# Diagonal blocks and score order of a chunked RWKV-7 layer: 8 steps of blocks instead of 16, and one more score per step in place of four ahead of the first

## The chip, the cores and the metric

One core of a Trainium2 chip runs the whole program in one launch. The metric is the device time of that launch in microseconds. Every product is made on TensorE (PE) from fp32 operands; VectorE (DVE), ScalarE (ACT) and GpSimd (POOL) do the elementwise work, and SyncE (SP), ScalarE and GpSimd issue DMAs.

## The reference, cut to what matters

Two trunk layers over 1024 latent and 256 context tokens of width 1024: an even layer (RWKV-7 time mixing in both directions with 12 heads of 64, and a Fourier mix), then an odd layer (retention). The change touches only the RWKV recurrence of the even layer:

```
def step(s, inp):
    r_t, w_t, k_t, v_t, kk_t, b_t = inp
    sa = jnp.einsum('bhij,bhj->bhi', s, kk_t)
    s = s * w_t[:, :, None, :] - sa[..., None] * b_t[:, :, None, :] + v_t[..., None] * k_t[:, :, None, :]
    return s, jnp.einsum('bhij,bhj->bhi', s, r_t)
...
for d in range(2):
    s_ctx, yc = rwkv7_scan(*tc[:6], zeros, d == 1)
    _, yl = rwkv7_scan(*tl[:6], s_ctx, d == 1)
```

## The kernel before, in words

The recurrence is computed in chunks of 64 tokens. With 1280 tokens there are 20 chunks, and the 12 heads in two directions are cut into three groups, so there are 60 steps. A step works on four `x` (two directions, two pairs of heads) of two heads each. What a step needs is prepared earlier by phase A and stored in DRAM: `AR` and `BK` (operands), `VT` (values), `PC` (decays), `Y0` (a bonus term), `G` (gates).

For each step `s`:

- `scores(s)` (L1121, products at L1127) multiplies `BK` by `AR` into the PSUM tiles `psc`; `masked(s)` (L1129) masks them on VectorE into a tile `scr`. Loads of `arr` and `bkp` come from `load_ops` (L1091).
- The 64x64 triangular system of each head is solved by the inverses of its two 32x32 diagonal blocks and a correction between them. `diag(s)` (L1138) stores the diagonal blocks of two steps from `scr` to the DRAM tile `dn`; `gather(s)` (L1179) loads them into a tile `tl`, one block to a partition.
- `inv(m)` (L1208) inverts all 128 blocks of the eight steps 8m to 8m+7 at once, in 31 rows of a product (L1218) and a sum (L1220) each. For m=0 these run on VectorE, for all others on GpSimd. It then stores the result twice (`dz`, and transposed as `dx`, with a copy at L1225 between).
- `bring(q, ...)` (L1232) loads the inverses of four steps back on SyncE, `dx` into `scr` and `dz` into `zs`.
- In step s-1, `offd1` (L1244, product at L1252) and `offd2` make the correction for step s from `scr` and `zs`.
- In step s, TensorE makes `wu` (L1496), ScalarE copies it to `wt` (L1497), a second product, the update of the state (L1529 to L1535, where VectorE scales by `pc`) and the output `pyo` (L1542) follow. TensorE runs in program order, so whatever it waits for holds all that is written behind it.

Scores are made ahead of the steps: in each step one score of a later step (L1515), up to 19 steps ahead, and in the steps listed in `CU` a second one (L1570, `more`).

Before the first step there is the last piece of phase A, the gate projections (tiles 20 to 25). The generator of phase B runs beside them: scores of steps 0 to 7, then `blocks(s)` (L1161) for s = 8, 10, ..., 22. `blocks` computes only the diagonal 64x64 products of two steps, from `dka` and `dkb` (loaded by `blocks_load`, L1154, on SyncE), so that the inverses of m=1 and m=2 can run before the full scores of those steps exist. ScalarE copies the 32x32 blocks to `dg` and stores them to `dn`. `both()` (L1364) places rows of the inverses beside the gate products: m=0's on VectorE, m=1's on GpSimd.

Behind the gates come, in this order, the bring-back of m=0, the loads for step 0, four scores (steps 8 to 11, `PR` = 4, with `bky` as their operand tile and `psg` as extra PSUM), and the steps. The rows of an inverse are placed by ticks: `slot(j)` is called four times a step and emits 2, 1, 1 and 1 rows; a gather follows its last store by three ticks (`TD`), the rows follow the gather by two (`WT`). `rows_until(s + 1)` at the start of a step emits whatever rows and bring-backs that step's correction still needs. GpSimd also runs the output norms (`norm`, L1277): the power L1296 and the product L1298, five norms to a group of 20 steps.

These lines set the places that the change edits:

```
for s in range(E, EB, 2):
    blocks(s)
    both()
    yield
...
if ivs and st.tick >= ivs[0][2]:
    row()
...
if s in CU:
    more(s)
slot(3)
```

Of the kernel before, what the change touches and what calls it, by code (L numbers as in the profile page):

```python
# [10 lines left out]
F32 = mybir.dt.float32  # L11
# [12 lines left out]
NB = 3  # L24
# [15 lines left out]
AG = 1  # L40
AL = {43:(42,),44:(43,),45:(44,),46:(42,),47:(43,),48:(45,),49:(42,),50:(43,),51:(45,),52:(42,),53:(43,),54:(45,),55:(42,),56:(43,),57:(42,),58:(43,)}
NR = 2
CU = (1, 2, 3, 4, 5, 7, 9)
PR = 4
EB = 24
EP = 2
EZ = 1
ER = (2,1,2)
# [9 lines left out]
NY = 6  # L58
TT = 1
TS = 7  # L60
RW = (2,1,1,1)
# [963 lines left out]
def phaseB(g):  # L1025
    nc, tc = g.nc, g.tc
    mm = nc.tensor.matmul
# [23 lines left out]
    E = 8  # L1051
    PES, ACTS, DVES = "tensor", "scalar", "vector"
    H = [slice(0, 64), slice(64, 128)]
# [3 lines left out]
    PSC = [ps2.tile([128, 512], F32, name=f"psc{h}") for h in range(2)]  # L1057
# [23 lines left out]
    ex = ee.enter_context(tc.tile_pool(name="exB", bufs=1, reuse_waits="tile"))  # L1081
# [6 lines left out]
    def gtile(name):  # L1088
        return tail.gen.tile([128, 512], F32, tag="gen", name=name)

    def load_ops(s, bk=None):  # L1091
        if 0 <= s < NS:
            AR[s] = ARR[s % (L + 3)]
            st.q.dma_start(AR[s], g.D["AR"][s // 20][:, s % 20])
            BK[s] = BKP[s % NB] if bk is None else bk
            nc.sync.dma_start(BK[s], g.D["BK"][s // 20][:, s % 20])
# [57 lines left out]
    def blocks_load(s):  # L1154

        if s < EB:
            DA[s], DB[s] = (ex.tile([128, 2, 4, 64], F32, tag=t, name=f"{t}{s}", bufs=2) for t in ("dka", "dkb"))
            for o, n in ((DA, "AR"), (DB, "BK")):
                nc.sync.dma_start(o[s], g.D[n][s // 20][:, s % 20 : s % 20 + 2, :, 0:64])

    def blocks(s):  # L1161

        spread(s)
        c = s % 8
        for j in range(2):
            for x in range(4):
                for h in range(2):
                    mm(PSC[h][0:64, 256 * j + 64 * x : 256 * j + 64 * x + 64], lhsT=DB[s][H[h], j, x], rhs=DA[s][H[h], j, x], start=True, stop=True, tile_position=(64 * h, 0))
        dg = ex.tile([64, 2, 4, 2, 32], F32, tag="dg", name=f"dg{s}", bufs=2)
        for b in range(2):  # L1170
            bs = slice(32 * b, 32 * b + 32)
            for h in range(2):
                nc.scalar.copy(dg[bs, :, :, h].rearrange("p c x t -> p (c x) t"), PSC[h][bs].rearrange("p (a t) -> p a t", t=64)[:, :, bs])
            nc.scalar.dma_start(DN[s // 8][b, 8 * c : 8 * c + 16].rearrange("u s t -> s u t"), dg[bs].rearrange("s c x h t -> s (c x h) t"))
        if c % 4 == 2:
            dgs.append((s + 1, st.tick + TD))
        blocks_load(s + 4)

    def gather(s):  # L1179

# [169 lines left out]

    for s in range(NB):
        load_ops(s)
    for _ in range(EW):
        yield
    for s in range(E):
# [16 lines left out]
        else:  # L1372
            rows(EP)

    blocks_load(E)
    blocks_load(E + 2)
    for s in range(E, EB, 2):
        blocks(s)
        both()
# [65 lines left out]
    def more(s, ps=None):  # L1445

        if ns <= min(s + L, NS - 1):
            if s >= 0:
                fetch(s)
            scores(ns, ps)  # L1450
            scored(ps)
# [3 lines left out]
        bring(*back.pop(0))  # L1455
    load_v(0)
    load_late(0)

    while nl < E + PR:
        load_ops(nl, st.pd.tile([128, 2, 256], F32, tag="y", name=f"bky{nl}", bufs=NY).rearrange("p q t -> p (q t)").rearrange("p (x t) -> p x t", t=128))  # L1460
        nl += 1
    while back and back[0][0] < 2:
        bring(*back.pop(0))
    load_group(0)
    for i in range(PR):
        more(-1, [gtile(f"psg{i}_{h}") for h in range(2)] if i % 2 else None)
        if i == NB:
            st.q = nc.sync
            for nl in range(nl, nl + NB):
                load_ops(nl)  # L1470
            nl += 1
            st.q = nc.scalar
        rows(RW[i % 4])
    st.q = nc.sync
    rows_until(0)
    offd1(0)
# [774 lines left out]
```

## Time and profile before

| | us |
|---|---|
| median of 3 runs (lowest, highest) | 1906.62 (1893.33, 1909.16) |
| the profiled execution's own time | 1908.86 |
| its span in the profile | 1907.1 |
| TensorE busy in the span | 1721.7 (90%) |
| VectorE, ScalarE, GpSimd busy | 992.4, 707.8, 743.4 |
| stretch with the diagonal blocks | 618 to 650 |
| gates and first inverse to the end | 650 to 681 |
| space before the first step | 681 to 708 |
| the 60 steps | 708 to about 1155 |

The times of single operations come from the profiled execution, whose own time is 2.24 us above the median of the runs. The span is shorter than its time by 1.8 us, which lie around it. A step is counted from its copy at L1497 to that of the next step.

### The profile page before, as it was taken

The numbers are of one execution on the slowest core, as the hardware profiler recorded it, in microseconds if no ns is written. First come the engines' busy times: TensorE is split into PE (matmuls) and PEld (weight loads), VectorE is DVE, ScalarE is ACT, GpSimd is POOL, SyncE is SP. The second block draws the span as 40 slices with busy tenths as digits, with TensorE's granted clock in tenths as the row PEclk, the third lists the DMA queues.
The fourth block names the chain that finished last, engine by engine and source line by source line (L and its number), as shares of the span: only waits on it lengthen the run. The fifth ranks groups of instructions, "written<-read, shape, count | busy, mean of one in ns | idle before, by whom it ended". The sixth has DMA issues, their size and how long they took to land.

```text
span 1907.1 us, 40211 instructions
## 1 busy us (share of the span) xinstructions
PE 1721.7 (90%) x16706; PEld 1460.4 (77%) x16706; DVE 992.4 (52%) x1532; ACT 707.8 (37%) x1570; POOL 743.4 (39%) x827
## 2 busy tenths in 40 slices
PE   6999998989787858898888888999999999999898
PEld 4777776777665747787877766779899898898776
DVE  6532589888986455545452334553442433524543
ACT  5322454545431314565555454343221222212321
POOL 4331344444342285088778411122442414414300
PEclk9999999999889979999897887999999999999999
DMA  9562265546548777688776664432111101101162
GB/s 317 172 223 73 74 182 141 155 136 175 131 137 264 164 190 224 175 223 217 202 187 169 160 161 144 143 122 84 45 45 36 55 23 56 56 23 56 51 204 99
DMA packets 343370, 261.90 MB, mean 137 GB/s; under 512 B 110396, under 2 KB 293172, under 8 KB 342932
## 3 DMA queue, kind: packets, MB, share of 16 engines
q1 hardware_dynamic: 319252, 222.88, 41.5%
q10 hardware_dynamic: 19536, 20.72, 3.8%
q0 software_dynamic: 4400, 15.73, 2.3%
q8 instruction: 132, 2.16, 0.5%
q14 instruction: 50, 0.41, 0.1%
HBM read 181.36 MB, written 77.91 MB: 136 GB/s over the span
## 4 chain that ended last, share of the span: by engine, by line
PE 45%; POOL 7%; issue 5%; DMA 5%; DVE 5%; ACT 2%; SPq 0%; ACTq 0%; POOLq 0%; DVEq 0%
PE pv L1905 6%; PE pg L1849 5%; PE pq L1849 5%; PE pk L1849 5%; PE pow_oo L1644 4%; PE pow_eo L1644 3%; POOL zz L1220 2%; POOL tp L1218 2%; PE psc L1127 2%; PE pst L1995 2%; PE wu L1496 1%; DMA br<-scr_BK 1%; PE inc L1252 1%; PE pkc L1849 1%; PE wu L1510 1%
## 5 line engine op out<-in xcount | busy, mean ns | idle before, releaser
L533 PE MATMUL pgm<-hh,wh 128*128 128x512 f32 (+1 forms) x624 | 171.8, 385 | 0.0
L511 POOL TENSOR_TENSOR wl<-wr,wh 128x512 fp32r<-128x512 f32 x60 | 86.8, 1451 | 212.0 <-ACT wh L509 198.0
L533 PE MATMUL pgm<-hl,wh 128*128 128x512 f32 (+1 forms) x624 | 162.0, 369 | 0.0
L533 PE MATMUL pgm<-hh,wl 128*128 128x512 f32 (+1 forms) x624 | 161.6, 368 | 0.0
L1218 POOL TENSOR_TENSOR tp<-zz,tl 128x60 f32<-128x60 f32 (+23 forms) x217 | 111.4, 513 | 47.8 <-DMA tl<-dn 31.8
L1220 POOL TENSOR_TENSOR zz<-zz,tp 128x60 f32<-128x60 f32 (+23 forms) x217 | 119.8, 552 | 17.0
L533 PEld LDWEIGHTS pgm<-hl,wh 128*128 128x128 f32 x624 | 108.1, 197 | 20.5 <-POOL hl L469 0.7
L533 PEld LDWEIGHTS pgm<-hh,wl 128*128 128x128 f32 x624 | 107.9, 196 | 19.7
L533 PEld LDWEIGHTS pgm<-hh,wh 128*128 128x128 f32 x624 | 104.9, 198 | 21.0 <-issue 6.2
L1905 PE MATMUL pv<-wv,hh 128*128 128x256 f32 x640 | 117.2, 285 | 0.0
L556 DVE SCALAR_TENSOR_TENSOR m<-pgm,dv,m 128x255 f32<-128x255 f32 (+2 forms) x108 | 105.2, 987 | 11.2 <-ACT m L546 8.4
L1532 DVE TENSOR_TENSOR inc<-inc,state 128x256 f32<-128x256 f32 x54 | 23.4, 433 | 158.4 <-PE inc L1529 57.6
L1905 PEld LDWEIGHTS pv<-wv,hh 128*128 128x128 f32 x640 | 99.5, 192 | 0.1
L1133 DVE TENSOR_TENSOR scr<-psc,mask 128x512 f32<-128x512 f32 x116 | 74.3, 682 | 35.2 <-PE psc L1127 35.2
L1644 PE MATMUL pow_eo<-w_eo,yhw_eo 128*128 128x512 f32 x320 | 90.5, 404 | 0.4 <-ACT w_eo L1610 0.3
L1905 PE MATMUL pv<-wv,hl 128*128 128x256 f32 x320 | 90.5, 283 | 0.0
L1127 PE MATMUL psc<-arr,bkp 64*64 64x128 f32 x1792 | 71.2, 286 | 10.7 <-DVE scr L1133 5.6
L1296 POOL TENSOR_TENSOR rv<-rv,mhalf 128x8 f32<-128x8 f32 x15 | 24.8, 1652 | 138.6 <-DVE rv L1295 84.9
L820 POOL TENSOR_TENSOR ar<-m,Pp 128x640 f32<-128x640 f32 (+2 forms) x30 | 36.6, 1228 | 95.6 <-ACT Pp L812 91.0
L1644 PE MATMUL pow_oo<-w_oo,yhw_oo 128*128 128x512 f32 x256 | 73.6, 404 | 0.1
L1644 PEld LDWEIGHTS pow_eo<-w_eo,yhw_eo 128*128 128x128 f32 x320 | 60.8, 192 | 16.0 <-ACT w_eo L1610 1.1
L1849 PE MATMUL pg<-hh,wg 128*128 128x512 f32 x256 | 72.1, 393 | 0.0
(348 smaller groups left out, 4305.0 us busy)
## 6 DMA issues: line engine op xcount, KB each, us to landing
aw<-ada_w SPq DMA_DIRECT2D x16, 1024.0 KB, 10.4
wr<-w_ev SPq DMA_DIRECT2D x60, 256.0 KB, 4.1
scr_AR<-ar SPq DMA_DIRECT2D x24, 640.0 KB, 3.7
scr_BK<-bk SPq DMA_DIRECT2D x24, 640.0 KB, 4.5
br<-scr_BK ACTq DMA_DIRECT2D x60, 256.0 KB, 4.1
arr<-scr_AR SPq DMA_DIRECT2D x56, 256.0 KB, 4.4
bkp<-scr_BK SPq DMA_DIRECT2D x56, 256.0 KB, 4.0
x<-xin SPq DMA_DIRECT2D x20, 512.0 KB, 6.3
```

Of the source, the lines that this page charges most:

```text
L511: nc.gpsimd.tensor_tensor(out=wl, in0=wr, in1=wh.bitcast(F32), op=ALU.subtract)
L533: g.nc.tensor.matmul(ps[:, b, :n], lhsT=st[:, k % 4, :], rhs=mv[:, k, c0 : c0 + n], start=(k == 0 and i == 0), stop=(k == 7 and i == 2))
L556: nc.vector.scalar_tensor_tensor(out=o, in0=i, scalar=g.muc[:, q, ft : ft + 1], in1=o, op0=ALU.mult, op1=ALU.add)
L820: nc.gpsimd.tensor_tensor(out=ar[:, cs, 64:128], in0=ch(proc(self.r, d, lo, n)), in1=Pp[:, cs, 1:65], op=ALU.mult)
L1127: mm(ps[h][H[m], 128 * x : 128 * x + 128], lhsT=BK[s][H[h], x, H[m]], rhs=AR[s][H[h], x, :], start=True, stop=True, tile_position=(64 * h, ...
L1133: tt(out=out, in0=p.rearrange("p (d q t) -> p d q t", d=2, q=2), in1=K["mask2"].unsqueeze(2).broadcast_to([128, 2, 2, 128]), op=ALU.mult)
L1218: eng.tensor_tensor(out=tv, in0=ZZ[:, 0:k, s : s + 1].broadcast_to([U, k, n]), in1=TL[:, s : s + 1, s + 1 : 32].broadcast_to([U, k, n]), o ...
L1220: eng.tensor_tensor(out=zo, in0=zo, in1=tv, op=ALU.add)
L1644: self.g.nc.tensor.matmul(ps[:, 512 * b : 512 * b + 512], lhsT=st[:, k, :], rhs=mv[:, 512 * b : 512 * b + 512], start=(k == 0 and i == 0), ...
L1849: mm(ps[:, 512 * b : 512 * b + n], lhsT=st[:, k, :], rhs=mv[:, k, o : o + n], start=(k == 0 and i == 0), stop=(k == 7 and i == 2))
L1905: mm(ps[:, 256 * e : 256 * e + 256], lhsT=st[:, k, c0 : c0 + 128], rhs=mv[:, k, :], start=(k == 0 and i == 0), stop=(k == 7 and i == 2))
L1995: mm(ps[:, 128 * (i - i0) : 128 * (i - i0) + 128], lhsT=o.kz[d][:, t], rhs=o.v[:, t], start=True, stop=True)
```

## The change

`EB` goes from 24 to 16, so that `blocks` runs for s = 8, 10, 12, 14 only (m=1). The blocks of m=2 (steps 16 to 23) now come from the scores themselves, by `diag`, as those of all later steps do. `PR` and its loop go, with the `bky` and `psg` tiles; the scores of steps 8 to 11 are made inside the steps, as `CU` now holds 0 to 10 instead of 1, 2, 3, 4, 5, 7 and 9. In `blocks` the four 64x64 quadrants of the array take one head and one step each, where before the two steps followed each other in one half of the columns; `dg` is 128 partitions wide, two copies of 128x256 take the place of four of 32x256, and four stores that of two. The loads of blocks 8 and 10 are issued by SyncE ahead of the first scores; those of blocks 12 and 14 by ScalarE behind the stores.

```diff
-CU = (1, 2, 3, 4, 5, 7, 9)
-PR = 4
-EB = 24
+CU = tuple(range(11))
+EB = 16
...
-                nc.sync.dma_start(o[s], g.D[n][s // 20][:, s % 20 : s % 20 + 2, :, 0:64])
+                st.q.dma_start(o[s], g.D[n][s // 20][:, s % 20 : s % 20 + 2, :, 0:64])
...
+        for x in range(4):
+            for h in range(2):
+                for j in range(2):
+                    mm(PSC[h][H[j], 64 * x : 64 * x + 64], lhsT=DB[s][H[h], j, x], rhs=DA[s][H[h], j, x], start=True, stop=True, tile_position=(64 * h, 64 * j))
+        dg = ex.tile([128, 4, 2, 64], F32, tag="dg", name=f"dg{s}", bufs=2)
+        for h in range(2):
+            nc.scalar.copy(dg[:, :, h], PSC[h][:, 0:256].rearrange("p (x t) -> p x t", t=64))
         for j in range(2):
-            for x in range(4):
-                for h in range(2):
-                    mm(PSC[h][0:64, 256 * j + 64 * x : 256 * j + 64 * x + 64], lhsT=DB[s][H[h], j, x], rhs=DA[s][H[h], j, x], start=True, stop=True, tile_position=(64 * h, 0))
-        dg = ex.tile([64, 2, 4, 2, 32], F32, tag="dg", name=f"dg{s}", bufs=2)
-        for b in range(2):
-            bs = slice(32 * b, 32 * b + 32)
-            for h in range(2):
-                nc.scalar.copy(dg[bs, :, :, h].rearrange("p c x t -> p (c x) t"), PSC[h][bs].rearrange("p (a t) -> p a t", t=64)[:, :, bs])
-            nc.scalar.dma_start(DN[s // 8][b, 8 * c : 8 * c + 16].rearrange("u s t -> s u t"), dg[bs].rearrange("s c x h t -> s (c x h) t"))
+            for b in range(2):
+                u0, r0 = 8 * (c + j), 64 * j + 32 * b
+                nc.scalar.dma_start(DN[s // 8][b, u0 : u0 + 8].rearrange("u s t -> s u t"), dg[r0 : r0 + 32, :, :, 32 * b : 32 * b + 32].rearrange("s x h t -> s (x h) t"))
         if c % 4 == 2:
             dgs.append((s + 1, st.tick + TD))
+        st.q = nc.scalar
         blocks_load(s + 4)
+        st.q = nc.sync
...
     for s in range(NB):
         load_ops(s)
+    blocks_load(E)
+    blocks_load(E + 2)
     for _ in range(EW):
         yield
...
-    blocks_load(E)
-    blocks_load(E + 2)
     for s in range(E, EB, 2):
         blocks(s)
         both()
...
-    while nl < E + PR:
-        load_ops(nl, st.pd.tile([128, 2, 256], F32, tag="y", name=f"bky{nl}", bufs=NY).rearrange("p q t -> p (q t)").rearrange("p (x t) -> p x t", t=128))
+    for _ in range(NB):
+        load_ops(nl)
         nl += 1
     while back and back[0][0] < 2:
         bring(*back.pop(0))
     load_group(0)
-    for i in range(PR):
-        more(-1, [gtile(f"psg{i}_{h}") for h in range(2)] if i % 2 else None)
...
-        rows(RW[i % 4])
     st.q = nc.sync
     rows_until(0)
     offd1(0)
```

In SyncE's order between the first inverse and the first step, the kernel before has four `bky` loads behind the first value load `vu0` and ahead of the bring-back of steps 4 to 7 (`scr4`, `scr6`, `zs1`) and the decays `pc0`:

```order
L1104 DMA vu0_5632<-scr_VT_61 64x1024
L1096 DMA bky8_5637<-scr_BK_65 128x512
L1096 DMA bky9_5640<-scr_BK_65 128x512
L1096 DMA bky10_5643<-scr_BK_65 128x512
L1096 DMA bky11_5646<-scr_BK_65 128x512
L1237 DMA scr4_4620<-dx0_5511 32x16x32
L1237 DMA scr6_4621<-dx0_5511 32x16x32
```

At the same place of SyncE's order the changed kernel has the loads of the three `bkp` tiles:

```order
L1103 DMA vu0_5509<-scr_VT_61 64x1024
L1095 DMA bkp2_4609<-scr_BK_65 128x512
L1095 DMA bkp0_4607<-scr_BK_65 128x512
L1095 DMA bkp1_4608<-scr_BK_65 128x512
L1239 DMA scr4_4620<-dx0_5398 32x16x32
L1239 DMA scr6_4621<-dx0_5398 32x16x32
```

Three loads stand where four stood; the bring-back and the `pc0` loads stay behind them.

In GpSimd's order, the kernel before ends m=2's inverse (`zz1`, then `dz2`, the copy to `tl2`, `dx2`) ahead of the first norm of step 10 (`rv0_0`, `cg0_0`), and m=3 begins behind that norm:

```order
L1220 TENSOR_TENSOR zz1_4631<-zz1_4631,tp1_4633 128x31
L1224 DMA dz2_6302<-zz1_4631 128x1024
L1225 COPY tl2_4626<-zz1_4631 64x32x32
L1227 DMA dx2_6305<-tl2_4626 64x1024
L1296 TENSOR_TENSOR rv0_0_7076<-rv0_0_7076,mhalf_77 128x8
L1298 TENSOR_TENSOR cg0_0_6990<-cg0_0_6990,rv0_0_7076 128x512
L1213 MEMSET zz1_4631 128x1024
```

In the changed kernel the same norm stands on GpSimd amid m=2's inverse, which reads `tl2`:

```order
L1220 TENSOR_TENSOR tp1_4633<-zz1_4631,tl2_4626 128x220
L1222 TENSOR_TENSOR zz1_4631<-zz1_4631,tp1_4633 128x10x22
L1298 TENSOR_TENSOR rv0_0_6901<-rv0_0_6901,mhalf_77 128x8
L1300 TENSOR_TENSOR cg0_0_6803<-cg0_0_6803,rv0_0_6901 128x512
L1220 TENSOR_TENSOR tp1_4633<-zz1_4631,tl2_4626 128x231
L1222 TENSOR_TENSOR zz1_4631<-zz1_4631,tp1_4633 128x11x21
```

Ten of the 31 rows of m=2 now stand ahead of the norm and 21 behind it, then `dz2`, the copy and `dx2`. Further on, the norm `rv0_512` stands behind 14 rows of m=3 (21 before) and `rv0_768` behind 29 of them (behind `dx3` before).

## Rows read from the trace of the kernel before

**Rows 1.** Windows, 618 to 650 us: busy of each engine, TensorE's clock, DMA share, GB/s
```profile
618.00:650.00 32.00, 24.30 (x313) 19.67 (x314) 6.66 (x20) 11.33 (x34) 1.28 (x1) 0.89 0.93 202
```

**Rows 2.** Timeline of TensorE, diagonal blocks (start, duration, idle before and its releaser)
```profile
622.53 1.77 PE L1168 MATMUL psc<-dka,dkb 64*64 64x64 f32 x32 [5.02 <-DMA dkb<-scr_BK]
...
638.38 1.15 PE L1168 MATMUL psc<-dka,dkb 64*64 64x64 f32 x32 [2.09 <-DMA dkb<-scr_BK]
...
648.52 1.15 PE L1168 MATMUL psc<-dka,dkb 64*64 64x64 f32 x32 [0.38 <-DMA dkb<-scr_BK]
```

**Rows 3.** Timeline of ScalarE, a pair of copies of one diagonal block
```profile
644.74 0.63 ACT L1173 COPY dg<-psc 32x256 f32<-32x256 f32 x2 [0.38 <-ACT dg L1173]
```

**Rows 4.** Timeline of VectorE, a gate amid the first inverse, and the inverse's last operation
```profile
649.15 0.69 DVE L601 SCALAR_TENSOR_TENSOR gth<-gth,pgb 128x512 f32<-128x512 f32 x1 [3.76 <-ACT gth L600]
...
680.51 0.21 DVE L1220 TENSOR_TENSOR zz<-zz,tp 128x31 f32<-128x31 f32 x1
```

**Rows 5.** Timeline of TensorE, the first of the four scores ahead of step 0
```profile
698.03 1.98 PE L1127 MATMUL psc<-arr,bky 64*64 64x128 f32 x32 [20.46 <-DMA bky<-scr_BK]
```

**Rows 6.** Timeline of SyncE, the issue of the two pc loads
```profile
700.75 1.25 SPq L1114 DMA_DIRECT2D pc<-scr_PC  x2
```

**Rows 7.** Timeline of ScalarE, the copy of wu, one per step: steps 1, 6 to 10, 15, 18, 23
```profile
713.31 0.37 ACT L1497 COPY wt<-wu 128x256 f32<-128x256 f32 x1
...
753.39 0.37 ACT L1497 COPY wt<-wu 128x256 f32<-128x256 f32 x1 [1.13 <-DMA bkp<-scr_BK]
...
759.57 0.37 ACT L1497 COPY wt<-wu 128x256 f32<-128x256 f32 x1 [0.22 <-PE wu L1496]
...
767.47 0.37 ACT L1497 COPY wt<-wu 128x256 f32<-128x256 f32 x1 [2.79 <-PE wu L1496]
...
772.78 0.37 ACT L1497 COPY wt<-wu 128x256 f32<-128x256 f32 x1 [0.21 <-PE wu L1496]
...
784.31 0.37 ACT L1497 COPY wt<-wu 128x256 f32<-128x256 f32 x1 [6.43 <-PE wu L1496]
...
814.37 0.37 ACT L1497 COPY wt<-wu 128x256 f32<-128x256 f32 x1 [0.20 <-PE wu L1496]
...
837.12 0.37 ACT L1497 COPY wt<-wu 128x256 f32<-128x256 f32 x1 [0.82 <-PE wu L1496]
...
866.86 0.37 ACT L1497 COPY wt<-wu 128x256 f32<-128x256 f32 x1 [1.28 <-PE wu L1496]
```

**Rows 8.** Timeline of GpSimd, end of m=2's inverse, two norms, m=3's inverse
```profile
744.92 0.53 POOL L1227 DMA_DIRECT2D dx<-tl  x1 [0.29 <-POOL tl L1225]
792.39 1.67 POOL L1296 TENSOR_TENSOR rv<-rv,mhalf 128x8 f32<-128x8 f32 x1 [46.94 <-DVE rv L1295]
...
810.56 0.24 POOL L1218 TENSOR_TENSOR tp<-zz,tl 128x31 f32<-128x31 f32 x1 [14.28 <-DMA tl<-dn]
...
820.98 0.60 POOL L1218 TENSOR_TENSOR tp<-zz,tl 128x231 f32<-128x231 f32 x1
...
826.74 0.66 POOL L1218 TENSOR_TENSOR tp<-zz,tl 128x255 f32<-128x255 f32 x1
...
838.65 1.65 POOL L1296 TENSOR_TENSOR rv<-rv,mhalf 128x8 f32<-128x8 f32 x1 [1.61 <-DVE rv L1295]
...
841.38 0.59 POOL L1218 TENSOR_TENSOR tp<-zz,tl 128x220 f32<-128x220 f32 x1
...
852.09 0.27 POOL L1220 TENSOR_TENSOR zz<-zz,tp 128x31 f32<-128x31 f32 x1
...
855.65 0.53 POOL L1227 DMA_DIRECT2D dx<-tl  x1 [0.29 <-POOL tl L1225]
```

**Rows 9.** DMA issues by transfer: count, size of each, median us from issue to landing
```profile
scr<-dx SPq DMA_DIRECT2D x30, 64.0 KB, 5.5
...
dx<-tl POOLq DMA_DIRECT2D x6, 256.0 KB, 4.0
...
pc<-scr_PC SPq DMA_DIRECT2D x6, 20.0 KB, 3.5
```

More of the change, by code (lines that the diff above doesn't have):

```diff
@@ L1464, in phaseB @@
     load_group(0)
-    for i in range(PR):
-        more(-1, [gtile(f"psg{i}_{h}") for h in range(2)] if i % 2 else None)
[L1467 to L1472, printed above, removed]
-        rows(RW[i % 4])
     st.q = nc.sync
```

## The prediction

> **What bounds the kernel now.** I read the busy times in windows first. In the 32 us in which the kernel before computes its diagonal blocks (618 to 650), TensorE is busy for 24.30 us, the DMA engines for 0.93 of the time, VectorE for only 6.66 us [rows 1]. Then TensorE's timeline of that stretch: block 8 waits 5.02 us and the block at 638.38 waits 2.09 us, both for a `dkb` load, while a block itself takes 1.15 us or somewhat more [rows 2]. So the blocks stage runs at the pace of its loads. ScalarE's rows show the other cost of a block: a pair of copies takes 0.63 us and the pair before held it for 0.38 us [rows 3]. VectorE shows what the stage ends with: the first inverse (m=0, steps 0 to 7) still waits 3.76 us for a gate at 649.15, and then runs nearly without a gap to 680.72 [rows 4]. Nothing of the RWKV steps can start before that inverse.
>
> Behind it, TensorE idles for 20.46 us until the `bky` loads land, and then makes four scores (steps 8 to 11) before the first step [rows 5]; SyncE issues the two `pc` loads only at 700.75 [rows 6]. Then I read the start of each step from ScalarE's copy of `wu` (L1497), one row per step: a step with a second score takes 7.90 us (step 7: 767.47 - 759.57), one without takes 5.31 to 6.18 (steps 8 and 6) [rows 7]. Last I read GpSimd: m=2's inverse (steps 16 to 23) hands over its result at 744.92 and is needed in step 15 (814.37), so it has 69 us in hand; m=3's runs from 810.56 to 852.36 and is needed in step 23 (866.86) [rows 7, 8]. The slack of m=2 is what the change spends.
>
> **Blocks and gates: -9 us.** Four blocks (16 to 22) go with their loads and copies. TensorE loses four blocks of at least 1.15 us, 4.6 us (638.38 is the first of the four, 648.52 the last), and the 2.09 and 0.38 us of waits among them; the loads of blocks 8 and 10 are issued before the first scores, which takes the 5.02 us [rows 2]. That is 12.1 us. Against it: blocks 12 and 14 are loaded by ScalarE behind two copies and four stores of their predecessor, so that the load is asked for later; I charge 2 us, the size of the wait at 638.38. Left: 10.1. The inverse on VectorE moves with the gates that its rows stand between, so its start moves by as much, but its later part is bare work (649.76 to 680.72) that no gate shortens, and GpSimd's m=1 starts earlier beside it and slows it sooner; I take 9 of the 10.1. Bounds: 15 if the wait of 3.76 us goes too [rows 4], 3 if the loads are as late as now. The four-at-a-time form itself I cost at nothing: the trace has 32 matmuls to a block [rows 2] and the changed kernel as many.
>
> One rule speaks against this term. The trace has the DMA engines at 0.93 busy there [rows 1]. By the Trainium skill, "DMA: Bandwidth & Descriptors", section "Issuing engines are not separate DMA queues", transfers started by ScalarE or SyncE run on the same 16 engines, and another issuer saves only issue time. By it the loads of blocks 12 and 14 gain nothing from ScalarE; the sum would lose the 5.02 us only where the loads were issued earlier, which for block 8 they are. The trace cannot yet say which holds for 12 and 14.
>
> **Prelude: -5 us.** The four scores and their `bky` loads leave the space between the inverse and step 0. Step 0 could then start some 10 us earlier, but its update waits for `pc`, which SyncE still issues behind the bring-back of the inverses. In its queue four `bky` loads go and three `bkp` loads come; so `pc` moves by a microsecond or two at most against the inverse, and lands 3.5 us after its issue in the list of DMAs [rows 9], near 704. Before, step 1 starts at 713.31 [rows 7], 32.6 us behind the inverse. With `pc` at 704 and the update and product behind it I get about 27. So -5 (-9 if `pc` is not last, -2 if step 0's new second score stands in the way).
>
> **Second scores in steps 6, 8, 10 (and 0): +6 us.** Step 7 with two costs 7.90; step 6 without costs 6.18 and step 8 5.31 [rows 7]: +1.7 and +2.6, and the mean of them for step 10, 6.5 in all, of which I take 6. Step 0's stands in the term above. Bounds 3 and 8.
>
> **m=2 comes late: +16 us.** Scores 16 to 23 are now made in steps 4 to 7, stored, gathered on SyncE in steps 6 and 8, and m=2's rows stand in GpSimd's order from step 8 on. Count from the start of step 8. The first row can run at about 11 us (mask, store and gather, and two landings of about 4 us). But ten rows on, GpSimd's order has the norm `rv0_0`, which used to stand behind the whole inverse. It starts 792.39 - 784.31 = 8.1 us after step 10 begins, and step 10 begins 784.31 - 767.47 = 16.8 us after step 8, now 19.4 with step 8's second score: 27.5. Ten rows take 820.98 - 810.56 = 10.4 us, so they are done at 21.6 and GpSimd waits 5.9 us. A norm then takes 841.38 - 838.65 = 2.7 us (30.2), the other 21 rows 852.36 - 820.98 less the norm and its wait of 4.3 = 27.1 us (57.3), the copy 3.3 us until `dx` is issued (855.65), landing 4.0 and the bring-back 5.5 [rows 8, 9]: 70.1. Step 15's off-diagonal product (L1252) wants it 814.37 - 767.47 = 46.9 us after step 8, plus some 4.8 for the second scores and 0.4: 52. It waits 18 us, and TensorE's order has all of step 15 behind it. I take 16, since loads catch up in the pause (step 6 waited 1.13 us for a `bkp` load, [rows 7]). Bounds 3 (the gather early, no wait at the norm, landings short) and 22.
>
> **m=3 behind it: +9 us.** GpSimd goes from m=2 straight to m=3, which starts as far ahead of step 16 as before, but two norms now stand differently: `rv0_512` behind 14 of its rows (21 before), and `rv0_768` before its end (behind it before). The first is ready only 838.65 - 837.12 = 1.5 us after step 18 begins. From there: 2.7, then 17 rows of 852.36 - 826.74 - 4.3 = 21.3, the second norm 2.7, then 3.3 + 4.0 + 5.5: 41 us after step 18 begins. Step 23 wants it at 866.86 - 837.12 + 0.4 = 30.1 [rows 7 to 9]. That is 11 us; the same working for the kernel before gives 28, so it just fitted. I take 9; bounds 0 and 13. Later inverses wait for their norms at the same steps as before, so I add nothing.
>
> **Sum.** -9 - 5 + 6 + 16 + 9 = +17 on the profiled execution of 1908.86 us, or 1926; the median of the runs is 2.2 us lower than that execution, so 1923.6, given as 1923. A measurement of this kernel tells about 1% (19 us) from no change: the bounds are 1887.6 and 1925.7.
>
> **Rivals.** (1) m=2 is in time: GpSimd takes the norm without a wait, step 15 waits 3 us and step 23 not at all. -9 - 5 + 6 + 3 = -5, 1902. For it: in steps 8 to 15 GpSimd has little else to do, it idled 46.94 us there [rows 8]. Against: the inverse alone needs 50 us with its copy and landings, and the norm stands in it. (2) In time, and the gates give back all: -15 - 9 + 4 = -20, 1887. For it: the 5.02 and 20.46 us waits are long [rows 2, 5]. (3) Slower: the pauses at steps 15 and 23 spread. The bring-back stands in SyncE's queue ahead of the step's `arr`, `bkp` and `vu` loads, so while it waits for `dx` they wait too. The price is a load's landing, 4 to 5 us, once more behind each pause, so +17 + 10 = +27, 1934. It decides once step 15 waits longer than the two to three steps of loads that are in hand, some 15 us. (4) The change does in the gates little of what it seems to, because loads bound them as before (the term's low bound, 3): +17 + 6 = +23, 1930.
>
> **How the numbers follow.** The forecast 0.42, rival 1 0.20, rival 2 0.08, rival 3 0.20, rival 4 0.10. Faster by over 1%: rival 2, and little else, 0.09. Slower by over 1%: rivals 3 and 4 and a third to a quarter of the forecast's own spread (it lies only 3 us under the bound), 0.38. Within: 0.53. The range takes the low bounds of the terms short of rival 2, 1896, to the high ones short of their joint sum, 1942.
>
> **What would show it.** In the changed profile: block 8 without a wait, and the first inverse ending near 671; step 1 near 699; in step 15 a wait of L1254 (the same product there) of 10 us or more put down to `scr<-dx`, GpSimd idle before `rv0_0`; a second such wait in step 23. If step 15 runs without a wait, the m=2 term falls and the kernel comes out near 1902. If the first inverse still ends near 680, the gates term falls.

## The result, and the profile after

The changed kernel takes 1917.32 us (median of 20 runs, 1908.95 to 1933.85), the kernel before in the same comparisons 1901.13 us (20 runs, 1887.63 to 1913.64). The ratio is 1.0098, with a 95% interval of 1.0074 to 1.0121: slower by about 16 us, just inside the 1% that the prediction called no change. Forecast were +17 us and 1923.

The two profiled executions differ by only 4.7 us in span (1911.8 against 1907.1), because phase A, whose code is the same, ended 13.8 us earlier in the second. So every stage below is counted from the last `pbo` product of phase A (at 584.19 before, at 570.37 after); each mark is a row's start less that. Line numbers of the changed kernel are one to three off in `blocks` and in the inverse, and eight less in the steps: `wt` is copied at L1489, the off-diagonal product is L1254, the norm is L1298 and L1300.

| mark | before | after | difference | of it in this stage | forecast for the stage |
|---|---|---|---|---|---|
| first inverse done (copy of `tl`) | 96.6 | 91.3 | -5.3 | -5.3 | -9 |
| step 1 | 129.1 | 123.2 | -6.0 | -0.7 | -5 |
| step 8 | 183.3 | 184.0 | +0.7 | +6.7 | +2 |
| step 16 | 240.5 | 255.7 | +15.3 | +14.6 | +20 (16 and two second scores) |
| step 24 | 291.2 | 313.5 | +22.3 | +7.1 | +9 |
| end of the span | 1322.9 | 1341.4 | +18.5 | -3.8 | 0 |

TensorE's timeline of the scores and blocks answers to [rows 2]: a late fourth score, then the four blocks.

```profile
593.91 1.99 PE L1126 MATMUL psc<-arr,bkp 64*64 64x128 f32 x32 [4.03 <-DMA bkp<-scr_BK]
...
609.25 0.69 PE L1167 MATMUL psc<-dka,dkb 64*64 64x64 f32 x32
...
611.79 0.69 PE L1167 MATMUL psc<-dka,dkb 64*64 64x64 f32 x32
...
617.60 1.13 PE L1167 MATMUL psc<-dka,dkb 64*64 64x64 f32 x32 [3.19 <-DMA dkb<-scr_BK]
...
622.77 0.69 PE L1167 MATMUL psc<-dka,dkb 64*64 64x64 f32 x32 [1.37 <-DMA dkb<-scr_BK]
```

Block 8 no longer waits, but a score before it does, and blocks 12 and 14 wait for loads that ScalarE issued. A block takes 0.69 us where it took 1.15. ScalarE's rows of one block (answering to [rows 3]) show the price:

```profile
613.70 0.65 ACT L1170 COPY dg<-psc 128x256 f32<-128x256 f32 x2 [3.07 <-DMA dn<-dg]
614.38 2.37 ACTq L1174 DMA_DIRECT2D dn<-dg  x4
616.78 0.46 ACTq L1158 DMA_DIRECT2D dka<-scr_AR  x1
617.29 0.59 ACTq L1158 DMA_DIRECT2D dkb<-scr_BK  x1
```

The copies have become cheap (0.65 us for all of a block), but six DMA issues now hold ScalarE's queue for 3.4 us (2.9 in the other block with loads behind it), and the gate's activation stands behind them.

The prelude, on VectorE, SyncE and TensorE (answering to [rows 5, 6]):

```profile
688.92 0.85 DVE L1526 TENSOR_TENSOR vu<-inc,pc 64x256 f32<-64x256 f32 x2 [21.08 <-DMA pc<-scr_PC]
```

```profile
677.65 0.89 SPq L1239 DMA_DIRECT2D scr<-dx  x2
678.63 3.80 SPq L1244 DMA_DIRECT2D zs<-dz  x4
684.98 2.30 SPq L1113 DMA_DIRECT2D pc<-scr_PC  x2
```

```profile
690.87 0.44 PE L1126 MATMUL psc<-arr,bkp 64*64 64x128 f32 x4 [3.18 <-DVE scr L1132]
```

`pc` is issued 684.98 - 661.65 = 23.3 us behind the first inverse; before it was 700.75 - 680.76 = 20.0. VectorE waits for it, the mask of step 0's first score stands behind that wait in VectorE's order, and TensorE's second score of step 0 waits for the mask. Step 0, which began at 681.72, takes 11.8 us.

ScalarE's copies of `wu`, answering to [rows 7]: steps 1, 8, 15, 16, 18, 21, 22 and 24.

```profile
693.53 0.37 ACT L1489 COPY wt<-wu 128x256 f32<-128x256 f32 x1 [5.22 <-PE wu L1488]
...
754.36 0.37 ACT L1489 COPY wt<-wu 128x256 f32<-128x256 f32 x1 [2.44 <-PE wu L1488]
...
805.84 0.37 ACT L1489 COPY wt<-wu 128x256 f32<-128x256 f32 x1 [0.20 <-PE wu L1488]
826.11 0.37 ACT L1489 COPY wt<-wu 128x256 f32<-128x256 f32 x1 [0.21 <-PE wu L1488]
...
838.99 0.37 ACT L1489 COPY wt<-wu 128x256 f32<-128x256 f32 x1
...
856.45 0.37 ACT L1489 COPY wt<-wu 128x256 f32<-128x256 f32 x1
867.01 0.37 ACT L1489 COPY wt<-wu 128x256 f32<-128x256 f32 x1 [4.14 <-DMA br<-scr_BK]
...
883.90 0.37 ACT L1489 COPY wt<-wu 128x256 f32<-128x256 f32 x1 [0.22 <-PE wu L1488]
```

Step 15 takes 20.3 us (805.84 to 826.11), step 21 10.6. TensorE's waits in them say why:

```profile
819.23 0.92 PE L1254 MATMUL inc<-scr 64*64 64x32 f32 x13 [13.49 <-DMA scr<-dx]
...
865.64 0.65 PE L1307 MATMUL pgn<-ident,cg 128*128 128x128 f32 x4 [3.39 <-POOL cg L1300]
...
876.91 0.81 PE L1254 MATMUL inc<-scr 64*64 64x32 f32 x13 [2.13 <-DMA scr<-dx]
```

and GpSimd's timeline (answering to [rows 8]) shows the chain behind them:

```profile
770.24 0.23 POOL L1220 TENSOR_TENSOR tp<-zz,tl 128x31 f32<-128x31 f32 x1 [86.65 <-DMA tl<-dn]
780.93 1.66 POOL L1298 TENSOR_TENSOR rv<-rv,mhalf 128x8 f32<-128x8 f32 x1 [0.38 <-DVE rv L1297]
...
813.89 0.54 POOL L1229 DMA_DIRECT2D dx<-tl  x1 [0.30 <-POOL tl L1227]
...
840.09 1.67 POOL L1298 TENSOR_TENSOR rv<-rv,mhalf 128x8 f32<-128x8 f32 x1 [8.34 <-ACT y2p L1261]
...
862.82 1.65 POOL L1298 TENSOR_TENSOR rv<-rv,mhalf 128x8 f32<-128x8 f32 x1
...
870.08 0.54 POOL L1229 DMA_DIRECT2D dx<-tl  x1 [0.29 <-POOL tl L1227]
```

m=2's `dx` is issued 813.89 - 754.36 = 59.5 us after step 8 begins (the working gave 60.6), m=3's 870.08 - 838.99 = 31.1 us after step 18 (31.5). The second norm waits 8.34 us behind 14 rows of m=3 and the third stands behind 29 of them, both as the order showed.

### The profile page after: what moved, and what is told of

It is laid out like the page before. It is cut to its first block, busy times and chain, and to the rows that moved or that the text cites. A ratio compares the mean times of both kernels' runs of the same rounds, so it can differ in the third digit from the quotient of the medians.

```text
span 1911.8 us, 39890 instructions
## 1 busy us (share of the span) xinstructions
PE 1709.6 (89%) x16578; PEld 1449.0 (76%) x16578; DVE 980.2 (51%) x1532; ACT 700.0 (37%) x1546; POOL 743.8 (39%) x827
## 4 chain that ended last, share of the span: by engine, by line
PE 41%; POOL 9%; DVE 6%; issue 6%; DMA 6%; ACT 2%; SPq 1%; ACTq 0%; POOLq 0%; DVEq 0%
PE pv L1897 6%; PE pg L1841 5%; PE pq L1841 5%; PE pk L1841 5%; PE pow_oo L1636 4%; POOL zz L1222 3%; POOL tp L1220 3%; PE pow_eo L1636 3%; PE pst L1987 2%; PE psc L1126 1%; PE pkc L1841 1%; DMA br<-scr_BK 1%; PE wu L1488 1%; POOL rv L1298 1%; DMA scr<-ada_w 1%
## 5 line engine op out<-in xcount | busy, mean ns | idle before, releaser
L532 PEld LDWEIGHTS pgm<-hl,wh 128*128 128x128 f32 x624 | 107.0, 195 | 20.3 <-POOL hl L468 0.9
L1524 DVE TENSOR_TENSOR inc<-inc,state 128x256 f32<-128x256 f32 x54 | 23.4, 432 | 179.7 <-ACT scr L1199 61.2
L1126 PE MATMUL psc<-arr,bkp 64*64 64x128 f32 x1920 | 77.0, 286 | 25.5 <-DVE scr L1132 12.7
L1126 PEld LDWEIGHTS psc<-arr,bkp 64*64 64x64 f32 x1920 | 59.7, 141 | 33.7 <-DVE scr L1132 18.1
L1636 PEld LDWEIGHTS pow_eo<-w_eo,yhw_eo 128*128 128x128 f32 x320 | 61.1, 193 | 16.0 <-ACT w_eo L1602 0.9
L1841 PE MATMUL pq<-hh,wq 128*128 128x512 f32 x256 | 70.2, 391 | 0.0
```

The costliest lines, as they stand in the source:

```text
L532: g.nc.tensor.matmul(ps[:, b, :n], lhsT=st[:, k % 4, :], rhs=mv[:, k, c0 : c0 + n], start=(k == 0 and i == 0), stop=(k == 7 and i == 2))
L1126: mm(ps[h][H[m], 128 * x : 128 * x + 128], lhsT=BK[s][H[h], x, H[m]], rhs=AR[s][H[h], x, :], start=True, stop=True, tile_position=(64 * h, ...
L1524: tt(out=inc, in0=inc, in1=STS[s % 2], op=ALU.add)
L1636: self.g.nc.tensor.matmul(ps[:, 512 * b : 512 * b + 512], lhsT=st[:, k, :], rhs=mv[:, 512 * b : 512 * b + 512], start=(k == 0 and i == 0), ...
L1841: mm(ps[:, 512 * b : 512 * b + n], lhsT=st[:, k, :], rhs=mv[:, k, o : o + n], start=(k == 0 and i == 0), stop=(k == 7 and i == 2))
```

## The experiments

All are compared with the kernel before on the same chip. The ratios come from 4 to 12 runs each (20 for the changed kernel), so that their intervals are 9 to 30 us wide, and a difference from the changed kernel is one of two such ratios. The stages of their profiles, counted as above, say more of where the time is, but each comes from one execution. "1 to 8" is from the start of step 1 to that of step 8; "clock" is TensorE's granted clock in that stretch, as a share of full speed.

| kernel | ratio (95%) | inverse done | to step 1 | 1 to 8 | clock | 8 to 16 | 16 to 24 |
|---|---|---|---|---|---|---|---|
| before | 1 | 96.6 | 32.6 | 54.2 | 1.00 | 57.2 | 50.7 |
| changed | 1.0098 (1.0074 to 1.0121) | 91.3 | 31.9 | 60.8 | 0.95 | 71.7 | 57.8 |
| 16 steps of blocks | 1.0105 (1.0051 to 1.0159) | 106.7 | 29.9 | 57.2 | 0.96 | 58.0 | 57.8 |
| old prelude and scores | 1.0039 (1.0000 to 1.0077) | 92.1 | 33.6 | 56.1 | 1.00 | 63.9 | 53.3 |
| m=2 not waited for | 1.0086 (1.0045 to 1.0127) | 93.3 | 32.6 | 61.2 | 0.92 | 61.1 | 59.1 |
| before, quadrants | 0.9982 (0.9942 to 1.0022) | 99.9 | 33.1 | 54.1 | 0.98 | 55.2 | 53.7 |
| loads by SyncE | 1.0070 (1.0039 to 1.0102) | 91.0 | 32.1 | 61.3 | 0.93 | 74.1 | 56.5 |
| early gather | 1.0148 (1.0069 to 1.0227) | 92.4 | 31.2 | 62.8 | 0.95 | 70.6 | 57.6 |
| pc first | 1.0080 (1.0041 to 1.0120) | 95.8 | 26.5 | 56.7 | 1.00 | 72.5 | 55.5 |
| before, no prelude, pc first | 0.9986 (0.9943 to 1.0029) | 98.1 | 27.8 | 58.7 | 0.94 | 59.8 | 50.6 |
| late block loads | 1.0108 (1.0067 to 1.0150) | 93.9 | 31.1 | 63.7 | 0.90 | 72.6 | 59.6 |
| norms off GpSimd | 0.9959 (0.9931 to 0.9987) | 95.0 | 31.3 | 62.7 | 0.91 | 68.0 | 54.5 |
| no prelude, pc first, quadrants | 1.0008 (0.9978 to 1.0038) | 97.5 | 27.6 | 58.3 | 0.94 | 55.9 | 54.5 |
| no prelude, pc first, norms off | 0.9992 (0.9966 to 1.0018) | 98.6 | 28.2 | 55.3 | 1.00 | 59.6 | 59.9 |

The column of the inverse also tells how far one execution stands for a kernel: six kernels with the changed gates code lie between 91.3 and 95.8, 93.3 on the mean (changed, old prelude, m=2 not waited for, early gather, pc first, norms off); three with the old one lie between 96.6 and 98.6.

**16 steps of blocks again.**

```diff
-EB = 16
+EB = 24
```

> The changed kernel with EB = 24: the blocks of steps 16 to 23 are made beside the gates again, by the new block form, everything else as changed. Theory (the loss is m=2's late inverse on GpSimd, seen as 13.5 us in front of step 15's L1254 and 2.1 us in front of step 23's): both waits vanish, steps 8 to 15 take about 59 us instead of 71.8, and four more blocks cost some 4 to 8 us beside the gates; 14 to 20 us faster than the changed kernel, so some 1 to 6 us around the kernel before. Rival (the loss lies in the second scores and the loads they crowd together in steps 0 to 10): the waits at 15 and 23 go, but their place is taken by load waits, and the time stays within 6 us of the changed kernel, 11 to 16 us slower than before.

The waits at steps 15 and 23 went, and steps 8 to 16 fell by 13.7 us to 58.0, as the theory had it. But the kernel gained nothing: the four blocks cost 15.4 us beside the gates (11 against the latest of the six like kernels), not 4 to 8, so that the total fits the rival, for another reason than the rival's. With six issues of ScalarE to a block, four of the eight waited 1.6 to 4.2 us for loads (3.96, 1.63, 3.02, 4.24) and the gates came late with them. The kernel with quadrants and SyncE's loads (below) has its inverse done at 97.5 to 99.9: the difference of 7 to 9 us, in single executions, is what the early loads and ScalarE's issuing cost together.

**The old space before step 0, EB still 16.**

```diff
-CU = tuple(range(11))
+CU = (1, 2, 3, 4, 5, 7, 9)
+PR = 4
```

(and the loop of four scores back in its place)

> The changed kernel with the old space before step 0 and the old list of second scores (four scores ahead of step 0, CU = 1, 2, 3, 4, 5, 7, 9), EB still 16. Scores 16 to 23 are then made in steps 0 to 5 rather than 4 to 7, so m=2's inverse starts two to three steps (16 to 22 us) earlier. Theory (GpSimd's chain is late): step 15's wait of 13.5 us vanishes; the space before step 0 costs some 1 to 6 us more; in sum 8 to 14 us faster than the changed kernel, 2 to 8 us slower than before. Rival (what costs is that m=2's inverse is not made beside the gates, whichever step its scores stand in): the wait at step 15 stays above 8 us and the time is that of the changed kernel or slower.

Step 15's wait fell to 8.38 us, between the two. The kernel came out 7 us slower than before (0 to 15), as the theory had it, so a little over half of the loss was gone, while the wait stayed above 8 us, as the rival had it: an earlier m=2 helps, yet one made in the steps is still late.

**m=2's inverse is not waited for.**

```diff
-            back.append((2 * m + i, st.tick + st.wait, DZ, DX))
+            back.append((2 * m + i, st.tick + st.wait, *(st.inv1 if m in (2,) else (DZ, DX))))
+        if m == 1:
+            st.inv1 = DZ, DX
```

> The changed kernel, in which steps 16 to 23 take the inverse of m=1 in place of that of m=2 (the inverse of m=2 is still computed on GpSimd and stored, but nobody reads it): all work and all transfers stay, only the wait for m=2 goes. Theory (GpSimd runs m=2 and m=3 back to back, so that it is one chain up to step 23): step 15 loses its 13.5 us, but m=3's end hardly moves (some 5 us earlier, as its norms come earlier), and step 23 then waits about 10 us; the net gain is 4 to 8 us, 8 to 13 us slower than before. Rival (the wait at step 15 is the whole loss): 13 to 15 us faster than the changed kernel, equal to before within 3 us.

Step 15's wait fell from 13.49 to 4.57 us and not to nothing, since SyncE issues the bring-back only when step 15 begins, whatever it brings. Steps 8 to 16 took 10.6 us less; steps 16 to 24 took 1.3 us more. So the wait at step 15 is most of that stage's loss; that step 23 takes half of it back, as the theory had it, the profile does not show: step 23 had no wait for `dx`. The ratio's interval is 9 to 24 us slower than before. It leaves out the rival's total (equal to before within 3 us) and holds that of the theory (8 to 13), though not by the theory's way. Against the changed kernel the profile ends 10.6 us sooner behind phase A, the ratios differ by 2 us only, and their intervals overlap.

**The quadrants alone, in the kernel before.** The body of `blocks` from the change, all else as before.

> The kernel before with the new form of the blocks alone (four quadrants, two copies, four stores), all loads and steps as before, 16 steps of blocks. A block takes 0.69 us in the changed kernel's trace against 1.15 before: eight blocks, 3.7 us of products. Theory (the stage runs at the pace of the loads, and ScalarE's four stores take 1.8 to 2.7 us a block against 0.6): no gain, within 4 us of before. Rival (products and copies are what the stage waits for): the first inverse ends 4 us earlier and so does the kernel.

The first inverse ended 3.3 us later and the kernel within its interval of before. What the faster products save does not reach the end of the inverse, as predicted: blocks still waited for `dkb` loads, the first of them 5.01 us.

**The loads of blocks 12 and 14 by SyncE.**

```diff
-        st.q = nc.scalar
         blocks_load(s + 4)
-        st.q = nc.sync
```

> The changed kernel with the loads of blocks 12 and 14 issued by SyncE instead of ScalarE. In the changed kernel ScalarE asks for them only behind two copies and four stores (some 2.5 us after the block's products) and block 12 then waits 3.19 us, block 14 1.37 us. Theory (the place in ScalarE's queue makes them late): the two waits shrink to under 1.5 us together and the first inverse ends some 3 us earlier (91.2 us behind phase A's last products now, then 88); the kernel gains 2 to 4 us. Rival (the transfers themselves are late on shared DMA engines, whoever issues them): the waits stay within 1 us of 4.6, and nothing is gained.

Block 12's wait went from 3.19 to 0.50 us, block 14's stayed (1.29):

```profile
613.14 0.69 PE L1167 MATMUL psc<-dka,dkb 64*64 64x64 f32 x32 [0.50 <-issue]
616.75 0.69 PE L1167 MATMUL psc<-dka,dkb 64*64 64x64 f32 x32 [1.29 <-DMA dkb<-scr_BK]
```

So the place in ScalarE's queue made block 12 late: its `dkb` load was issued 3.8 us behind the start of block 8 by ScalarE and 1.6 us behind it by SyncE. The Trainium skill, "DMA: Bandwidth & Descriptors", section "Issuing engines are not separate DMA queues", says that another issuer saves issue time only. The run agrees as far as it goes: the issue came 2.2 us sooner, and the wait fell by 2.7. But the inverse ended at 91.0 against 91.3, so no gain is seen there, and the ratios (1.0070 and 1.0098) have intervals that overlap: the wait was not on the way to the inverse's end. Neither theory nor rival had both halves right.

**The gather of m >= 2 earlier.**

```diff
-            dgs.append((s, st.tick + TD))
+            dgs.append((s, st.tick + (1 if s >= E else TD)))
...
-            ivs.append((m, inv(m), st.tick + WT))
+            ivs.append((m, inv(m), st.tick + (0 if m >= 2 else WT)))
```

> The changed kernel with the gather of m >= 2 one tick behind its last store instead of three, and the rows allowed at once (for m=0 and m=1 as before). In the changed kernel SyncE issues m=2's last gather 8.6 us after step 8 begins and GpSimd's first row runs at 15.9 us. Theory (m=2's chain is set by its start): the first row comes 3 to 5 us earlier, the norm then costs GpSimd a wait of 2 to 4 us more in its middle, and step 15 waits 10 to 13 us instead of 13.5; the kernel gains 1 to 3 us. Rival (only the start counts, the norm in the middle costs nothing): the whole 3 to 5 us are gained at step 15.

GpSimd's first row came 7.0 us after step 8 begins instead of 15.9, but the norm then waited:

```profile
773.58 0.23 POOL L1220 TENSOR_TENSOR tp<-zz,tl 128x31 f32<-128x31 f32 x1 [80.43 <-DMA tl<-dn]
```

```profile
794.32 1.66 POOL L1298 TENSOR_TENSOR rv<-rv,mhalf 128x8 f32<-128x8 f32 x1 [3.19 <-DVE rv L1297]
```

The norm starts 27.7 us after step 8 begins (the prediction worked out 27.5), and step 15 still waits 10.34 us: 8.9 us at the start became 3.2 at the end. The kernel did not gain the 1 to 3 us of the theory: at a ratio of 1.0148 from four runs it is some 9.5 us slower than the changed kernel, with intervals that overlap. Two scores wait 3.2 and 3.5 us for `bkp` (1.8 and 3.0 in the changed kernel), yet step 24 begins only 1 us later than there, counted from phase A; the profile's loss is in steps 24 to 40 (124.4 us against 108.3), where TensorE waits 13.4 us for GpSimd's norms against 3.9.

**pc first.**

```diff
     load_v(0)
+    load_group(0)
     load_late(0)
...
-    load_group(0)
```

> The changed kernel with the two pc loads issued right behind the first value load, ahead of the bkp loads and of the bring-back of steps 4 to 7. In the changed kernel step 0 takes 11.8 us, as VectorE waits 21 us for pc until 688.92. Theory (pc is what holds step 1): step 0 falls to 6 to 8 us, step 1 begins some 5 us earlier, and the 5 us stay until step 15, where the wait for m=2 may take back little (its scores also come earlier): 4 to 6 us faster than the changed kernel. Rival (the br, arr or bkp loads behind it are as late): step 0 stays above 10 us.

From the inverse to step 1 it took 26.5 us instead of 31.9, and step 0 9.1 instead of 11.8; three more kernels with this edit took 27.6 to 28.2. So `pc` was what hid the prelude's gain. In the total it would be some 3 us (1.0080 against 1.0098), which the intervals do not show: step 15 still waits 12.95 us in place of 13.49.

**The kernel before without the prelude, pc first.** `EB` = 24, the old blocks and their loads, the change's `CU` and no scores ahead of step 0.

> The kernel before (16 steps of blocks beside the gates, old block form, SyncE's loads) without the four scores ahead of step 0, with second scores in steps 0 to 10 and pc first. Theory (the prelude's removal is worth 5 us once pc is out of the way; the second scores cost some 5 us; m=2's inverse is in time): step 1 begins 7 to 9 us earlier than before, no wait at steps 15 and 23, in sum 2 to 6 us faster than the kernel before. Rival (second scores crowd the loads of steps 0 to 10): steps 1 to 8 take 6 us more than before and nothing is left, within 2 us of before or slower.

Step 1 was 4.7 us nearer to the inverse (7 to 9 were expected), steps 1 to 8 took 4.6 us more (58.7; the rival had 6, and the granted clock was 0.94 there against 1.00), and the kernel was equal to before. Each half came with its sign and in part of its size; they cancel.

**The first block loads late again.**

```diff
-    blocks_load(E)
-    blocks_load(E + 2)
     for _ in range(EW):
         yield
...
+    blocks_load(E)
+    blocks_load(E + 2)
     for s in range(E, EB, 2):
```

> The changed kernel with the loads of blocks 8 and 10 back behind the scores (issued by SyncE where the kernel before has them). In the changed kernel block 8 has no wait, but the fourth score waits 4.03 us for bkp, whose load stands behind the four early block loads (issues of 2.3 to 3.1 us each). Theory (the early loads only move the wait): block 8 waits some 5 us, the score's 4 us vanish, the first inverse ends within 2 us of the changed kernel's 91.2 us behind phase A's last products, and the time stays within 3 us. Rival (the early loads are worth the 5 us that the prediction gave them): the inverse ends 4 to 5 us later and so does the kernel.

```profile
612.00 1.13 PE L1167 MATMUL psc<-dka,dkb 64*64 64x64 f32 x32 [5.05 <-DMA dkb<-scr_BK]
```

Block 8 waited its 5 us again, no score waited as long as 1 us, and the inverse ended at 93.9. That is 2.6 us later than in the changed kernel, and in the middle of the six like kernels: the early loads moved the wait, and no gain of theirs is shown. The kernel's time was that of the changed one, as the theory had it.

**The norms off GpSimd.**

```diff
-        nc.gpsimd.tensor_tensor(out=rv, in0=rv, in1=K["mhalf"].broadcast_to([128, 8]), op=ALU.pow)
+        nc.vector.reciprocal(rv, rv)
...
-        nc.gpsimd.tensor_tensor(out=xv, ...
+        nc.vector.tensor_tensor(out=xv, ...
```

> The changed kernel with the two norm operations of GpSimd (power and product) moved to VectorE, a reciprocal in place of the power -1/2, so that nothing but inverses stands in GpSimd's order in the steps. Theory (GpSimd's order of norms and rows carries part of the loss behind step 8): m=2 ends 2.7 us earlier and m=3 5 to 14 us earlier (no 8.3 us wait for the norm after 14 rows); step 15 waits about 10.5 us instead of 13.5, step 21 no longer waits for the norm that stands behind m=3's rows (10.6 us down to 6 to 7), step 23 does not wait for dx; steps 8 to 24 take 8 to 12 us less and the kernel is 6 to 12 us faster than the changed kernel. Rival (the inverses' length and start alone count): only the 2.7 us at step 15 come, step 21 stays above 9 us.

This kernel leaves out the square root: it scales by the reciprocal, where the power -1/2 stood. It was the largest effect of all: some 1.4% below the changed kernel by the two ratios, 0.4% below the one before. As the theory had it, step 21 fell from 10.6 to 5.9 us. Step 15 still waited 11.05 us and step 23 4.97, where the theory had no wait, so steps 8 to 24 took 7 us less and not 8 to 12. Most of the gain came where nobody had looked: from step 40 to step 59 it took 144.4 us, against 162.0 in the changed kernel and 161.0 before. There the windows (TensorE's busy time is the first behind the length, its granted clock the third from the end) and a row of the changed kernel show two parts:

```profile
992.23:1154.22 161.99, 131.52 (x2558) 112.35 (x2557) 50.98 (x135) 82.05 (x230) 81.37 (x127) 0.83 0.64 163
1007.07:1151.46 144.39, 123.52 (x2559) 104.89 (x2561) 58.06 (x147) 82.19 (x229) 61.49 (x107) 0.91 0.70 176
```

```profile
1030.30 1.12 PE L1307 MATMUL pgn<-ident,cg 128*128 128x128 f32 x4 [4.53 <-POOL cg L1300]
```

In the changed kernel TensorE waits four times there, 12.2 us in all, for a norm on GpSimd; these waits are gone, and its idle time falls by 9.6 us. The other 8.0 us are busy time of TensorE, at a granted clock of 0.91 against 0.83. That part is not shown to be the norms': the run with m=2 not waited for, whose code in these steps is the changed kernel's, had 0.90 there and took 152.7 us, and all kernels with the norms on GpSimd took 152.7 to 163.0.

**Two versions meant to beat both.** The first is the kernel without the prelude, with pc first and the quadrants.

> The kernel before with three of the change's parts: the four-quadrant blocks, no scores ahead of step 0, second scores in steps 0 to 10, and pc first; 16 steps of blocks and SyncE's loads stay. Theory (m=2 beside the gates is what has to stay; the issue of loads by ScalarE, not the quadrants, lengthens the blocks): the first inverse ends at 97 to 100 us behind phase A's last products (106.7 with ScalarE's loads), no waits for dx at steps 15 and 23, 2 to 8 us faster than before. Rival (the quadrants' four stores lengthen the blocks): the inverse ends above 103 us, and the kernel is slower than before by some 4 us.

The inverse ended at 97.5 with no wait for `dx`, as the theory had it, and the kernel was still equal to before. With pc first and no prelude, then, 8 steps of blocks come out at 1.0080, and 16 at 1.0008 and 0.9986: it is m=2's place that makes the changed kernel slower (the blocks' form and the place of their loads, in which these kernels differ too, showed no gain by themselves). The second adds the norms to the version with the old blocks:

```diff
-        nc.gpsimd.tensor_tensor(out=rv, in0=rv, in1=K["mhalf"].broadcast_to([128, 8]), op=ALU.pow)
+        nc.scalar.activation(rv, rv, AF.Sqrt)
+        nc.vector.reciprocal(rv, rv)
```

> The kernel of the fourth run of the second set (16 steps of blocks in the old form, SyncE's loads, no scores ahead of step 0, second scores in steps 0 to 10, pc first) with the norms taken off GpSimd: a square root on ScalarE, a reciprocal and the product on VectorE. Theory (norms and inverse rows in one queue on GpSimd cost time in all three groups of steps, most in steps 40 to 59, where the run with the norms off took 144 us instead of 162): m=2 in time and norms off GpSimd add up; the steps behind 40 take 144 to 150 us, 10 to 25 us faster than before. Rival (the gain of that run lay in its reciprocal, which ScalarE's square root with its table load and the extra handover gives back): steps behind 40 take 158 us or more, within 6 us of before.

It was equal to before: steps 40 to 59 took 157.9 us, and steps 16 to 24 59.9. In the table of groups, and in the timelines of ScalarE and TensorE, the square root shows what gave the gain back:

```profile
L1295 ACT ACTIVATE rv<-rv 128x8 f32<-128x8 f32 x15 | 3.1, 208 | 37.6 <-DVE rv L1294 37.6
```

```profile
1042.07 0.21 ACT L1295 ACTIVATE rv<-rv 128x8 f32<-128x8 f32 x1 [2.28 <-DVE rv L1294]
...
1042.74 0.64 PE L282 MATMUL padb<-scr,SL 128*32 128x128 f32 x16 [2.68 <-ACT zs L1274]
```

ScalarE stands 37.6 us, 2.5 us a norm, waiting for VectorE's sums, with the steps' copies queued behind it. In steps 40 to 59 TensorE waits 14.6 us for two of these copies (`zs` and `wt`), where it waited 1.0 us for them in the kernel before and 9.0 us for the norm on GpSimd: the wait changed its engine. No version that computes what the reference does was clearly faster than the kernel before.

## Why the prediction was right

The total was right (+17 forecast, +16.2 between the medians, +18.5 in the two profiles) and so was its main mechanism, but the terms were off by 2 to 5 us each. That these cancelled is luck, and so is part of the +18.5: steps 24 to 40, where the code is the same, took 4.8 us less than before, at a granted clock of 0.97 against 0.89.

- *Blocks and gates, -9:* measured -5.3 (-4.4 by the means of like kernels). The step that failed is that the 5.02 us of block 8 go with the early issue: a score ahead of it waited 4.03 us for a `bkp` load that now stands behind the block loads, and with late loads the inverse ended only 2.6 us later, within the spread. SyncE's queue was held by the four early block loads for 8.6 us (579.10 to 587.66, 0.47 to 3.05 us a load). The charge of 2 us for the loads of blocks 12 and 14 stood in 3.19 + 1.37 us of waits; with the first of them gone, the inverse ended no sooner (loads by SyncE). The quadrants at nothing: shown by the run with them alone.
- *Prelude, -5:* measured -0.7. The step that failed is that `pc` would move by a microsecond or two at most and land near 704 in the time of the old profile; it was issued 3.3 us later behind the inverse, and VectorE's order tied step 0's second score to it. With pc first and no prelude, four kernels took 26.5 to 28.2 us from the inverse to step 1, against 32.6 before: the 5 us are there once `pc` is out of the way. Why the bring-back ahead of `pc` was later is open.
- *Second scores, +6:* steps 1 to 8 took 6.7 us more where 2 were forecast. The term that was mis-sized left TensorE's clock out. The windows of steps 1 to 8, of the kernel before, the changed one and that with pc first:

```profile
713.31:767.47 54.16, 45.76 (x1234) 39.61 (x1232) 31.36 (x66) 24.73 (x70) 28.10 (x48) 1.00 0.74 220
693.53:754.36 60.83, 49.65 (x1266) 42.82 (x1267) 32.54 (x68) 24.68 (x71) 0.00 (x0) 0.95 0.71 204
696.53:753.22 56.69, 47.00 (x1266) 40.54 (x1265) 32.28 (x68) 24.72 (x70) 0.00 (x0) 1.00 0.78 225
```

  Of the 6.7 us, 3.9 are busy time of TensorE, in a stretch of which a part ran at the lower of the clock's two levels (the granted clock was 0.50 from 692.8 to 696.0 and from 750.9 to 754.1). The two kernels with the same second scores and a clock of 1.00 took 56.7 and 55.3 us, 2.5 and 1.1 over the kernel before and so near the forecast; the first of them has m=2's stores and gathers in its steps. The nine others had 0.90 to 0.96 and took 57.2 to 63.7 us. At 0.94 and 0.95, two without m=2's stores took 58.3 and 58.7, two with them 60.8 and 62.8, so that this traffic may have a share; its size is open.
- *m=2 late, +16:* with the two second scores 20 were forecast for steps 8 to 16, 14.6 measured. The chain on GpSimd was met to 1 us (59.5 against 60.6, the norm at 26.6 against 27.5). The term that was mis-sized is the landing of `dx` and its bring-back: 4.0 + 5.5 us by the medians, 819.23 - 813.89 = 5.3 measured (`dx` landed 2.9 us behind its issue). The wait was 13.49 us instead of 18. One step of the working held by luck: the first row came at 15.9 us, not 11, so that the norm waited 0.38 us and not 5.9, and both give the same end; the run with the early gather shows the norm as the next bound. (11 and 10.4 us make 21.4, not 21.6, which changes nothing.)
- *m=3 behind it, +9:* 7.1 measured, and `dx` at 31.1 us after step 18 (31.5 worked out). But it was paid in another place: 4.7 us in step 21, where TensorE waits 3.39 us for the norm behind m=3's rows, and only 2.13 us of wait for `dx` in step 23.

Of the rivals, the slower one (pauses that spread on SyncE) did not show: step 15's wait was 13.49 us, under the 15 it named, and step 16 took 6.4 us as before. The rival that the gates gain little was closest to what the gates did. The 46.94 us of idle GpSimd that the rival of an m=2 in time drew on lie ahead of the norm of step 10, from step 5 on, and not in steps 8 to 15.

## What to carry to other kernels

Before moving a long chain to a later start, count its engine's own order: each instruction of another job that stands amid it adds its own wait, so the chain ends when the latest of those is ready plus what stands behind it, and an earlier start may buy little. A load that is issued earlier pushes back what stood there before it; look for the wait in front of the next load in that queue. When a long prelude is cut, look for the small load that nobody waited for till then. Before a stage's difference is put down to traffic or waits, compare TensorE's busy time and granted clock in it with those of the other kernel.

## What the runs showed that was not expected

- Four quadrants: a block of 32 matmuls took 0.69 us against 1.15 with two halves of the array, at the same count and shape (64x64).
- Six DMA issues of ScalarE to a block took 3.4 us (2.37 for four stores, 0.46 and 0.59 for two loads) in one block and 2.9 in another, against 0.31 us for each of two stores before.
- With the same instructions, steps 1 to 8 took 56.7 us at a granted clock of 1.00 and up to 63.7 at 0.90.
- Taking two operations of 1.65 and 1.05 us, fifteen times, off GpSimd, and leaving the root out, made the kernel some 26 us faster by the ratios. In the profile 17.6 us of it lie in steps 40 to 59, where the change did nothing: 9.6 less idle time, and 8.0 less busy time at a higher granted clock.
